# Hybrid decoder layer: the recurrence's tanh, exponentials and square roots laid in a row on ScalarE

## The chip, the cores and the metric

The kernel runs on one core of one Trainium2 chip. The metric is device time in microseconds (us), the median of the runs. Engines are named as in the profile: PE is TensorE, ACT is ScalarE, DVE is VectorE, POOL is GpSimd and SP is the engine that issues the DMAs.

## The reference

One decoder layer on a residual stream of 2048 tokens of width 1024, with 16 meta tokens put in front (T = 2064). Both groups of heads read one projection, and one output projection joins them:

```python
u = rmsnorm(h, pre_g)
q, k, v, g_att, x_lru, g_lru = split(u @ w_in)          # six blocks of 1024 columns
att = rmsnorm(stick_breaking_attention(q, k, v), att_out_g) * silu(g_att)
lru = rmsnorm(rglru_branch(x_lru, ...), lru_out_g) * silu(g_lru)
y = concatenate([att, lru]) @ w_out
return h + rmsnorm(y, post_g)

# rglru_branch: after a causal convolution of width 4 gives xc
r = sigmoid(gate_a(xc)); i = sigmoid(gate_x(xc))
log_a = 8 * r * log_sigmoid(lru_lambda)
a = exp(log_a)
b = sqrt(-expm1(2 * log_a)) * (i * xc)
h_t = a_t * h_(t-1) + b_t

# stick-breaking attention, 8 heads of 128
z = q k' / sqrt(128);  w = the product over later keys of sigmoid(-z), split at each key;  o = w v
```

## The kernel before, in words

The work goes through 8 rounds, called heads here, 0 to 7. Round h holds attention head h and block h of 128 recurrence channels. Products on TensorE are made of three f16 matmuls (high x high, high x low, low x high), and so every projection is evicted twice: ACT writes the high half (`kH`, `qH`, line 792), then DVE subtracts it and writes the low half (`kL`, `qL`, line 796).

A projection is cut in chunks of columns: for k and v 144, 384, 512, 512, 512, for q 128, 384, 512, 512, 512. A chunk is 24 matmuls into one PSUM bank `mm`, of which there are three (`psm`, with `bufs=3`, `Ring(3)` in the planner). A bank is free again when its low half has been written. The two gate matmuls of the recurrence (L379 and L380) and the small matmul that scales a weight (L152) use the same three banks.

Attention cuts the 16 query tiles of a head into 26 segments of up to 1024 key columns. Each goes through: scores on PE (`z`, L219, two PSUM buffers), sigmoid on ACT (L223), a mask on POOL (L228), a running product on DVE (L233), a high half on ACT (`w`, L243 and L245), a low half on DVE (L250 and L251), a DMA transpose into `wT`, and the output matmuls on PE (`o`, L270).

The mix of block c is the elementwise part of the recurrence. It works on two halves (m = 0, 1) of HT = 1032 columns each: `tanh` (L390), `exp_a` (L393), `exp_a2` (L397, in place of its own input) on ACT, `rest` on DVE (L402: (exp_a2 + 1) x tanh), `sqrt` on ACT (L406), `drive` on POOL (L410), `recur`, a scan, on DVE (L414), `square` on ACT (L418) and `add` on POOL (L424 for the first block, L426 for the others). Mix c starts after the 12 gate matmul pairs of block c, and from mix 1 on this falls into the time in which PE makes k and q of head c. Tanh and sigmoid are in one of ACT's tables here, the exponential in another and the square root in a third; a change between them is an instruction of its own, ACT_TABLE_LOAD.

The order on PE, ACT and DVE is written out beforehand by a planner (class `Plan`, function `weave`). It keeps a model time for each engine (`plan.free`), adds a modelled duration for each step (`A` for ACT, `V` and `SC` for DVE, `G` for POOL) and calls a step's function, which emits its instructions, when the model time of PE reaches the time that the step was put down for (`plan.at`). The order of the calls is the order on every engine, since each takes its instructions in order. The planner's own times are only its model; they set the order and nothing else.

Of the kernel before, what the change touches and what calls it, by code (L numbers as in the profile page):

```python
# [70 lines left out]
def hybrid_layer(nc, tc, I, out):  # L71
# [221 lines left out]
    HT = T // 2  # L293
# [325 lines left out]
    plan = Plan()  # L619
    A = lambda t, n, table=None: plan.run("act", t, 0.2 + n / 1200, table)  # L620
# [393 lines left out]
    def gate_in(c, m, k, t):  # L1014
        def go():
            head[c]["mix"].gate_in(m, k)
            t2 = V(A(max(t, plan.free["pe"]), 344), 400)
            urgent.append((t2 + 1.2, rmm, lambda: out(t2)))

        def out(t2):  # L1020
            mix = head[c]["mix"]
            def emit():
                mix.gate_out(m, k)
                t3 = PE(0, 2 * 344)
                rcs[k % 2].put(t3)
                t4 = A(A(t3, 344, "sig"), 344, "sig")
                rmm.put(t4)
                if k == 5:
                    G(t4, HT)
                head[c]["gates"] += 1  # L1030
                if k + 2 < 6:
                    plan.at(t3, lambda: gate_in(c, m, k + 2, t3))
                if head[c]["gates"] == 6 and "conv1" in head[c]:
                    plan.at(t4, head[c].pop("conv1"))
                if head[c]["gates"] == 12:
                    plan.at(t4, lambda: rows_for(len(mix.xs), lambda: mix_end(c)))
            emit()
        rcs[k % 2].get(go)
# [4 lines left out]
    def mix_end(c):  # L1043
        mix = head[c]["mix"]
        n = len(mix.xs)
        now = lambda: plan.free["pe"]

        def tanh(m):
            mix.tanh(m)
            t = A(now(), HT, "tanh")  # L1050
            plan.at(t, (lambda: tanh(m + 1)) if m + 1 < n else (lambda: exp(0)))

        def exp(i):
            m = i // 2
            (mix.exp_a2 if i % 2 else mix.exp_a)(m)
            t = A(now(), HT, "exp")
            if i % 2:
                plan.at(t, lambda: rest(m))
            if i + 1 < 2 * n:
                plan.at(t, lambda: exp(i + 1))  # L1060

        def rest(m):
            mix.rest(m)
            t = V(now(), HT)
            rrow.put(t)
            if m + 1 == n:
                plan.at(t, lambda: sqrt(0))

        def sqrt(m):
            mix.sqrt(m)  # L1070
            t = A(now(), HT, "sqrt")
            plan.at(t, lambda: drive(m))
            if m + 1 < n:
                plan.at(t, lambda: sqrt(m + 1))

        def drive(m):
            mix.drive(m)
            t = G(now(), HT)
            plan.at(t, lambda: recur(m))

        def recur(m):
            mix.recur(m)
            t = SC(now(), HT)
            rlrow.put(t)
            if m + 1 == n:
                head[c]["hs"] = mix.xcs
            plan.at(t, lambda: square(m))

        def square(m):
            mix.square(m)  # L1090
            t = A(now(), HT)

            def add():
                mix.add(m)
                rrow.put(G(t, HT))
            plan.at(t, add)
        tanh(0)


    wos, nout, held, first_out = [], [0], [], []  # L1100
# [421 lines left out]
```

## Time and profile before

| what | value |
|---|---|
| time, median of 3 runs | 1884.48 us (1883.8 to 1887.8) |
| the profiled execution's own time | 1882.98 us |
| its span, first to last instruction | 1881.1 us |
| mean granted TensorE clock | 0.989 |
| busy: PE, DVE, ACT, POOL | 95%, 68%, 56%, 18% of the span |
| ACT_TABLE_LOAD | 46, of 1.283 us each |
| DMA | 108 GB/s on average |

The profiled execution is 1.5 us below the median of the runs and 0.8 us below the fastest of the three; what is read from its rows holds for its own 1882.98 us. Busy shares are means over stages with different limits. An engine's idle time has a cost only where PE waits for it, so the waits of PE are what is looked for.

### The profile page before, as it was taken

What the parts mean: (1) busy time and instruction counts of PE and PEld (TensorE: products, weight loads), DVE (VectorE), ACT (ScalarE), POOL (GpSimd) and SP (SyncE); (2) the same over time, 40 slices, a digit from 0 to 9 for tenths busy, and PEclk for the clock granted to TensorE, in tenths of its full rate; (3) what the DMA queues carried; (4) which work ended last, traced back from release to release, by engine and by line L of the source; (5) the groups of instructions that cost most, each with busy time, mean ns of one, the idle gap of its engine ahead of it and who ended that gap; (6) DMA issues with size and microseconds to landing.
All of it is one profiled execution on the core that took longest, in us unless ns stands there. A gap on an engine that the chain in (4) does not pass through costs nothing. (4 is left out here: it accounts for less than half of the span.)

```text
span 1881.1 us, 30861 instructions
## 1 busy us (share of the span) xinstructions
PE 1795.0 (95%) x12104; PEld 1155.2 (61%) x12104; DVE 1282.7 (68%) x1759; ACT 1047.9 (56%) x1789; POOL 343.3 (18%) x442
## 2 busy tenths in 40 slices
PE   3987999999999999998999899999999999999998
PEld 2544665566556655664665466556655678888776
DVE  8747876987778668767885788687857851134553
ACT  7768557556655755665567546665565742233221
POOL 0013012311320131014101401241131000002222
PEclk8998999999999999999999999999999999999999
DMA  6713650654175226433652355145405884354553
GB/s 211 144 29 74 125 109 27 123 105 87 49 139 104 63 54 127 97 64 65 134 100 55 73 126 98 46 97 132 83 30 108 192 184 144 96 177 154 179 190 134
DMA packets 428417, 203.46 MB, mean 108 GB/s; under 512 B 362976, under 2 KB 396768, under 8 KB 428272
## 3 DMA queue, kind: packets, MB, share of 16 engines
q1 hardware_dynamic: 428272, 201.49, 45.9%
q8 instruction: 95, 1.56, 0.3%
q14 instruction: 50, 0.41, 0.1%
HBM read 78.23 MB, written 34.08 MB: 60 GB/s over the span
## 5 line engine op out<-in xcount | busy, mean ns | idle before, releaser
L174 PE MATMUL mm<-uH,wH 128*128 128x512 f16 (+3 forms) x1808 | 616.3, 345 | 8.3 <-DVE sa L892 2.6
L174 PE MATMUL mm<-uL,wH 128*128 128x512 f16 (+3 forms) x1808 | 616.3, 345 | 0.0
L174 PE MATMUL mm<-uH,wL 128*128 128x512 f16 (+3 forms) x1808 | 615.4, 345 | 0.8 <-DVE wL L163 0.8
L174 PEld LDWEIGHTS <-wH 128*128 128x128 f16 x3616 | 333.9, 98 | 273.1 <-issue 10.4
L233 DVE TENSOR_TENSOR_SCAN row<-row 128x656 f32<-128x656 f32 (+6 forms) x208 | 352.4, 1695 | 131.9 <-POOL row L228 101.5
L174 PEld LDWEIGHTS <-wL 128*128 128x128 f16 x1808 | 177.3, 98 | 158.5 <-DVE wL L163 1.3
L270 PE MATMUL o<-wT,v 128*128 128x128 f16 x3392 | 224.4, 220 | 30.0 <-DMA wT<-w 26.5
L270 PEld LDWEIGHTS <-v 128*128 128x128 f16 x3392 | 206.1, 98 | 70.4 <-issue 27.0
L223 ACT ACTIVATE row<-z,zs 128x656 f32<-128x656 f32 (+6 forms) x208 | 171.5, 825 | 125.2 <-PE z L219 115.0
L251 DVE TENSOR_TENSOR w<-row,w 128x640 f16<-128x640 f32 (+5 forms) x208 | 179.8, 865 | 16.3 <-ACT w L245 14.4
L245 ACT CAST w<-row 128x640 f16<-128x640 f32 (+5 forms) x208 | 155.1, 746 | 51.8 <-DVE row L233 49.1
L537 PE MATMUL y<-woH,aH 128*128 128x512 f32 x352 | 140.8, 400 | 1.6 <-DVE w L251 1.6
L537 PE MATMUL y<-woH,aL 128*128 128x512 f32 x352 | 138.7, 394 | 0.5 <-DVE aL L530 0.5
L537 PE MATMUL y<-woL,aH 128*128 128x512 f32 x352 | 138.3, 393 | 0.6 <-DVE woL L490 0.6
L228 POOL TENSOR_SCALAR_AFFINE_SELECT row<-row 128x128 f32<-128x128 f32 x128 | 59.9, 469 | 406.4 <-ACT row L223 374.7
L219 PE MATMUL z<-kH,qH 128*128 128x328 f16 (+10 forms) x384 | 123.6, 322 | 0.6 <-ACT row L223 0.6
L219 PE MATMUL z<-kL,qH 128*128 128x328 f16 (+10 forms) x384 | 123.5, 322 | 0.0
L219 PE MATMUL z<-kH,qL 128*128 128x328 f16 (+10 forms) x384 | 123.4, 321 | 0.0
L219 PEld LDWEIGHTS <-qH 128*128 128x128 f16 x768 | 72.8, 98 | 56.3 <-issue 3.7
L369 DVE TENSOR_TENSOR cs<-lrow,cs 64x344 fp32r<-64x344 f32 x96 | 50.7, 528 | 78.5 <-ACT cs L368 71.3
L530 DVE TENSOR_TENSOR aL<-araw,aH 128x1024 fp32r<-128x1024 f32 x32 | 39.4, 1231 | 93.2 <-ACT aH L527 92.1
L1468 POOL TENSOR_TENSOR row<-row 128x512 f32<-128x512 f32 x32 | 46.5, 1454 | 262.9 <-ACT row L1467 251.1
(208 smaller groups left out, 2476.2 us busy)
## 6 DMA issues: line engine op xcount, KB each, us to landing
wraw<-in_w_in SPq DMA_DIRECT2D x45, 512.0 KB, 3.5
row<-in_x SPq DMA_DIRECT2D x22, 512.0 KB, 3.8
aa_d<-sa SPq DMA_DIRECT2D x34, 256.0 KB, 2.0
al_d<-sl SPq DMA_DIRECT2D x32, 256.0 KB, 2.4
araw<-in_w_out SPq DMA_DIRECT2D x16, 512.0 KB, 4.4
araw<-al_d SPq DMA_DIRECT2D x16, 512.0 KB, 4.3
yl_d<-ys SPq DMA_DIRECT2D x32, 256.0 KB, 2.1
row<-yl_d SPq DMA_DIRECT2D x16, 512.0 KB, 3.2
```

What stands on the lines that cost most here:

```text
L174: pe.matmul(out=ps[:, :n], lhsT=a[:, kt, :], rhs=b[:, kt, c0:c0 + n], start=(k == 0), stop=(k == 3 * KT - 1))
L219: pe.matmul(out=z[:, a, :n], lhsT=l[:, qs], rhs=r[:, c], start=(x == 0), stop=(x == 2))
L223: act.activation(out=self.om[:, :L].rearrange("p (a c) -> p a c", a=self.parts), in_=self.z[:, :self.parts, :self.n], func=AF.Sigmoid, sca ...
L228: pool.affine_select(out=d, in_=d, pattern=[[-1, P]], compare_op=ALU.is_gt, fill=1.0, base=0, channel_multiplier=1)
L233: dve.tensor_tensor_scan(out=om, data0=om, data1=om, initial=self.pred.om[:, 0:1] if self.si else WS, op0=ALU.mult, op1=ALU.bypass)
L245: act.copy(out=w[:, r0:r0 + nb * P], in_=om[:, self.m0:self.L])
L251: dve.tensor_tensor(out=w[:, r0 + nb * P:r0 + 2 * nb * P], in0=om[:, self.m0:self.L], in1=w[:, r0:r0 + nb * P], op=ALU.subtract)
L270: pe.matmul(out=o[:, c], lhsT=l, rhs=r, start=(self.si == 0 and x == 0), stop=(self.last and x == len(prods) - 1))
L369: dve.tensor_tensor(out=cs[oth, :n], in0=xc[own, a:a + n], in1=cs[own, :n], op=ALU.subtract)
L530: dve.tensor_tensor(out=aL, in0=raw, in1=aH, op=ALU.subtract)
L537: pe.matmul(out=ps, lhsT=a[:, c, :], rhs=b[:, 512 * half:512 * half + 512], start=(c == 0 and x == 0), stop=(c == KT - 1 and x == 2))
L1468: pool.tensor_tensor(out=yt[:, cs], in0=yt[:, cs], in1=pg[:, cs], op=ALU.mult)
```

## The change

The six steps of tanh and exponentials of a mix, which the planner emitted one at a time, each after the modelled end of the one before, are now emitted together: tanh of both halves, then both exponentials of both halves. The two square roots also follow each other at once, after the second half's `rest`. Nothing is added or taken out but table loads: by the built program there are 38 ACT_TABLE_LOAD where there were 46. The planner runs with the new steps, so its order differs everywhere from mix 0 on.

```diff
-        def tanh(m):
-            mix.tanh(m)
-            t = A(now(), HT, "tanh")
-            plan.at(t, (lambda: tanh(m + 1)) if m + 1 < n else (lambda: exp(0)))
-
-        def exp(i):
-            m = i // 2
-            (mix.exp_a2 if i % 2 else mix.exp_a)(m)
-            t = A(now(), HT, "exp")
-            if i % 2:
-                plan.at(t, lambda: rest(m))
-            if i + 1 < 2 * n:
-                plan.at(t, lambda: exp(i + 1))
+        def tables():
+
+            for m in range(n):
+                mix.tanh(m)
+                A(now(), HT, "sig")
+            for m in range(n):
+                mix.exp_a(m)
+                mix.exp_a2(m)
+                t = A(A(now(), HT, "exp"), HT)
+                plan.at(t, lambda m=m: rest(m))
 
         def rest(m):
             mix.rest(m)
             t = V(now(), HT)
             rrow.put(t)
             if m + 1 == n:
-                plan.at(t, lambda: sqrt(0))
-
-        def sqrt(m):
-            mix.sqrt(m)
-            t = A(now(), HT, "sqrt")
-            plan.at(t, lambda: drive(m))
-            if m + 1 < n:
-                plan.at(t, lambda: sqrt(m + 1))
+                plan.at(t, sqrt)
+
+        def sqrt():
+            for m in range(n):
+                mix.sqrt(m)
+                t = A(now(), HT, "sqrt")
+                plan.at(t, lambda m=m: drive(m))
...
-        tanh(0)
+        tables()
```

On ACT in mix 0 (the first head, attention already running) the program had, from the first exponential on:

```order
L393 ACT_TABLE_LOAD
L393 ACTIVATE lrow<-row,nsp_m 128x1032
L223 ACT_TABLE_LOAD
L223 ACTIVATE row<-z,zs 128x528
L397 ACT_TABLE_LOAD
L397 ACTIVATE row<-row,nsp_m_76 128x1032
L161 ACTIVATE wH<-wraw,wm 128x1024
L243 CAST w<-row 128x2x16
L245 CAST w<-row 128x512
L393 ACTIVATE lrow<-row,nsp_m 128x1032
L223 ACT_TABLE_LOAD
L223 ACTIVATE row<-z,zs 128x656
```

It now has in that place:

```order
L393 ACT_TABLE_LOAD
L393 ACTIVATE lrow<-row,nsp_m 128x1032
L397 ACTIVATE row<-row,nsp_m_76 128x1032
L393 ACTIVATE lrow<-row,nsp_m 128x1032
L397 ACTIVATE row<-row,nsp_m_76 128x1032
L243 CAST w<-row 128x2x16
L245 CAST w<-row 128x384
L223 ACT_TABLE_LOAD
L223 ACTIVATE row<-z,zs 128x528
L161 ACTIVATE wH<-wraw,wm 128x1024
L406 ACT_TABLE_LOAD
L406 ACTIVATE row<-row 128x1032 x2
```

The four exponentials stand together. The first half of a segment's weights (`w`, 384 columns), which stood ahead of the first exponential, and the sigmoid of 528 columns, which stood behind it, now stand behind the fourth. Over the whole program mix 0 has 10 loads before and 4 now, mix 1 has 6 and 4, and mixes 2 to 7 have three each before and now.

On ACT in mix 4, from the last gate's sigmoids (L381, L382) on, before:

```order
L381 ACTIVATE row<-mm,pp 64x344
L382 ACTIVATE lrow<-mm,pp 64x344
L390 ACTIVATE row<-row,nsp 128x1032
L792 ACTIVATE kH<-mm 128x512
L390 ACTIVATE row<-row,nsp 128x1032
L792 ACTIVATE qH<-mm 128x128
L393 ACT_TABLE_LOAD
L393 ACTIVATE lrow<-row,nsp_m 128x1032
L792 ACTIVATE qH<-mm 128x384
L397 ACTIVATE row<-row,nsp_m_76 128x1032
L393 ACTIVATE lrow<-row,nsp_m 128x1032
L397 ACTIVATE row<-row,nsp_m_76 128x1032
```

And now:

```order
L381 ACTIVATE row<-mm,pp 64x344
L382 ACTIVATE lrow<-mm,pp 64x344
L390 ACTIVATE row<-row,nsp 128x1032 x2
L393 ACT_TABLE_LOAD
L393 ACTIVATE lrow<-row,nsp_m 128x1032
L397 ACTIVATE row<-row,nsp_m_76 128x1032
L393 ACTIVATE lrow<-row,nsp_m 128x1032
L397 ACTIVATE row<-row,nsp_m_76 128x1032
L792 ACTIVATE kH<-mm 128x512
L792 ACTIVATE qH<-mm 128x128
L792 ACTIVATE qH<-mm 128x384
L406 ACT_TABLE_LOAD
```

The evictions of the last k chunk (`kH`, 512 columns) and of the first two q chunks (`qH`, 128 and 384), which stood singly between the steps, now stand behind all six. Mixes 3, 5 and 7 have the same rows in this place now; in mix 6 the `kH` stands ahead of the six and a `qH` of 512 columns behind them; in mix 1 and mix 2 one `qH` of 512 columns stands first behind them.

On DVE in mix 4, from the low half of the k chunk before the last on, before:

```order
L796 SCALAR_TENSOR_TENSOR kL<-mm,kH 128x512
L195 TENSOR_SCALAR zs<-wm 128x1
L796 SCALAR_TENSOR_TENSOR kL<-mm,kH 128x512
L796 SCALAR_TENSOR_TENSOR qL<-mm,qH 128x128
L146 TENSOR_REDUCE wm<-wraw 128x1
L149 TENSOR_SCALAR dg<-identb,wm 128x128
L796 SCALAR_TENSOR_TENSOR qL<-mm,qH 128x384
L402 SCALAR_TENSOR_TENSOR row<-row 128x1032
```

And now:

```order
L796 SCALAR_TENSOR_TENSOR kL<-mm,kH 128x512
L195 TENSOR_SCALAR zs<-wm 128x1
L402 SCALAR_TENSOR_TENSOR row<-row 128x1032
L146 TENSOR_REDUCE wm<-wraw 128x1
L149 TENSOR_SCALAR dg<-identb,wm 128x128
L402 SCALAR_TENSOR_TENSOR row<-row 128x1032
L796 SCALAR_TENSOR_TENSOR kL<-mm,kH 128x512
L796 SCALAR_TENSOR_TENSOR qL<-mm,qH 128x128
L796 SCALAR_TENSOR_TENSOR qL<-mm,qH 128x384
```

The low half of the last k chunk stood ahead of both `rest` steps (L402), and now stands behind both. On PE the order of the chunks is the same in both programs there (last k chunk, then q of 128, 384, 512, 512, 512); behind the last gate pair stand 12 matmuls of the last k chunk before and 9 now in mix 4 (9 in mixes 3 and 5 too, 12 in mix 7). The first matmul of the first q chunk of 512 columns waits for the bank of the last k chunk, so for that chunk's `kL`, in both programs.

## Rows read from the trace of the kernel before

**Rows 1.** The page, section 1: busy us (share of the span) xinstructions of TensorE.

```profile
PE 1795.0 (95%) x12104; PEld 1155.2 (61%) x12104; DVE 1282.7 (68%) x1759; ACT 1047.9 (56%) x1789; POOL 343.3 (18%) x442
```

**Rows 2.** Busy time by stretch: us, busy us (x) per engine, clock, DMA.

```profile
850.00:950.00 100.00, 94.82 (x693) 56.18 (x692) 80.91 (x111) 52.82 (x102) 26.24 (x37) 1.00 0.52 104
```

**Rows 3.** Groups of ScalarE instructions: busy us, mean ns, idle before.

```profile
L223 ACT ACT_TABLE_LOAD x15 | 19.2, 1283 | 0.3
...
L406 ACT ACT_TABLE_LOAD x10 | 12.8, 1283 | 0.2
```

**Rows 4.** Timeline of ScalarE around mix 4: start us, us, instruction, idle before.

```profile
833.11 0.54 ACT L382 ACTIVATE lrow<-mm,pp 64x344 f32<-64x344 f32 x1
833.67 1.15 ACT L390 ACTIVATE row<-row,nsp 128x1032 f32<-128x1032 f32 x1
835.14 0.60 ACT L792 ACTIVATE kH<-mm 128x512 f16<-128x512 f32 x1 [0.32 <-PE mm L174]
...
836.97 1.28 ACT L393 ACT_TABLE_LOAD   x1
838.26 1.16 ACT L393 ACTIVATE lrow<-row,nsp_m 128x1032 f32<-128x1032 f32 x1
...
840.77 1.15 ACT L397 ACTIVATE row<-row,nsp_m 128x1032 f32<-128x1032 f32 x1
841.82 1.14 ACT L393 ACTIVATE lrow<-row,nsp_m 128x1032 f32<-128x1032 f32 x1
842.99 1.15 ACT L397 ACTIVATE row<-row,nsp_m 128x1032 f32<-128x1032 f32 x1
...
847.47 1.06 ACT L406 ACTIVATE row<-row 128x1032 f32<-128x1032 f32 x1
...
849.48 1.05 ACT L406 ACTIVATE row<-row 128x1032 f32<-128x1032 f32 x1
```

**Rows 5.** Timeline of VectorE around mix 4.

```profile
835.77 0.69 DVE L796 SCALAR_TENSOR_TENSOR kL<-mm,kH 128x512 f16<-128x512 f32 x1 [2.56 <-ACT kH L792]
...
837.19 1.21 DVE L146 TENSOR_REDUCE wm<-wraw 128x1 f32<-128x1024 f32 x1
...
841.95 1.23 DVE L402 SCALAR_TENSOR_TENSOR row<-row 128x1032 f32<-128x1032 f32 x1 [0.49 <-ACT row L397]
```

**Rows 6.** Timeline of TensorE: the first matmul of three projection chunks.

```profile
834.94 0.22 PE L174 MATMUL mm<-uH,wH 128*128 128x128 f16 x1
...
836.28 0.33 PE L174 MATMUL mm<-uH,wH 128*128 128x384 f16 x1
...
840.18 0.38 PE L174 MATMUL mm<-uH,wH 128*128 128x512 f16 x1
```

**Rows 7.** Timeline of GpSimd at the start of head 4.

```profile
857.72 3.84 POOL L426 TENSOR_TENSOR acc_l<-acc_l,row 128x1016 f32<-128x1016 f32 x1 [1.02 <-ACT row L418]
...
861.88 2.38 POOL L426 TENSOR_TENSOR acc_l<-acc_l,row 128x1032 f32<-128x1032 f32 x1
864.21 0.61 POOL L228 TENSOR_SCALAR_AFFINE_SELECT row<-row 128x128 f32<-128x128 f32 x2
```

**Rows 8.** Waits of TensorE, 500 to 1450 us: us in total, times, longest us.

```profile
PE o L270 <- DMA wT<-w: 15.2, 11, 2.8
PE o L270 <- ACT sq L285: 3.4, 1, 3.4
```

**Rows 9.** Busy time by stretch at the starts of heads 3 and 5.

```profile
700.00:704.40 4.40, 2.43 (x22) 1.41 (x21) 0.52 (x2) 0.69 (x2) 0.41 (x2) 1.00 0.50 98
704.40:707.80 3.40, 3.40 (x10) 1.20 (x9) 3.40 (x6) 1.99 (x5) 0.00 (x0) 0.50 0.00 0
...
1070.00:1085.00 15.00, 10.87 (x82) 6.25 (x81) 14.51 (x21) 10.18 (x21) 6.18 (x6) 1.00 0.73 131
```

**Rows 10.** Timeline of ScalarE in mix 0.

```profile
146.03 1.16 ACT L390 ACTIVATE row<-row,nsp 128x1032 f32<-128x1032 f32 x1 [1.25 <-DVE w L251]
...
151.49 0.70 ACT L223 ACTIVATE row<-z,zs 128x528 f32<-128x528 f32 x1
```

## The prediction

> **What bounds the kernel now.** The page's first section comes first: TensorE is busy for 95% of the span, ScalarE for 56%, VectorE for 68% [rows 1]. ScalarE, whose work the change rearranges, is therefore not the bound over the whole. To see whether it is one in a stage, read the busy time by stretch: in the first half of head 4 TensorE is busy for 94.82 of 100 us and ScalarE for 52.82 [rows 2]. So two questions decide. Where does TensorE wait now, and does the new order take such a wait away? And does it make a new one in a place where TensorE now runs through?
>
> **Table loads.** A load takes 1.283 us, whichever table it is [rows 3], and the instruction behind it starts at once: the load at 836.97 ends at 838.25, the exponential starts at 838.26 [rows 4]. Eight loads fewer are 8 x 1.283 = 10.3 us of ScalarE's time, all of it in mixes 0 and 1. In mixes 2 to 7 there are three loads before and three after, so there the change moves work and saves none. An engine that is 56% busy gives time to the end only where TensorE waits for it, and I book these 10.3 us as nothing by themselves; their cover is TensorE's own work in the first two heads. What they would be worth without it is a rival below.
>
> **The new stall, mixes 3, 4, 5 and 7.** The last k chunk is evicted by `kH` on ScalarE and `kL` on VectorE, and only `kL` gives back its bank, which the first q chunk of 512 columns takes again three chunks later. Before, `kH` stood between the two tanh (835.14) [rows 4], `kL` came at 835.77 [rows 5], and that q chunk started at 840.18 [rows 6] with the bank long free.
>
> Now `kH` stands behind all six activations. Taking mix 4's own times: the group starts at 833.67, where the first tanh does, right behind the last gate's sigmoid (833.11 + 0.54). Two activations in a row are 1.05 us apart when the second doesn't need the first (840.77 to 841.82), and 1.17 us when it does, as `exp_a2` needs `exp_a` (841.82 to 842.99); the last takes 1.15, the load 1.28 [rows 4]. So the group takes 1.05 + 1.15 + 1.28 + 1.17 + 1.05 + 1.17 + 1.15 = 8.0 us and ends at 841.7. `kH` (0.60) ends at 842.3. VectorE meanwhile has the first `rest` from 839.5, when the first `exp_a2` ends, the 1.21 us reduction of a weight, the second `rest` (1.23 each) [rows 5], and only then `kL`: 839.5 + 1.23 + 1.21 + 1.23 + 0.69 = 843.9.
>
> When does TensorE want the bank? A chunk of 384 columns is 24 matmuls and takes 840.18 - 836.28 = 3.90 us [rows 6], so TensorE does 24 x 384 / 3.90 = 2360 columns per us, and a matmul of 512 takes 0.217 us. With 9 instead of 12 k matmuls behind the last gate pair it arrives 0.65 us earlier than the old 840.18, at 839.5. It waits for 843.9 - 839.5 = 4.3 us in mixes 3, 4 and 5, and for 3.7 us in mix 7, which still has the 12. If `kL` is not held by the `rest` steps, the wait is until 842.3 + 0.69 = 843.0, 3.5 us; that is the lower bound. The upper bound has one more attention step of the size of a low half (0.69) ahead of `kL`: 5.0 us. In mix 6 `kH` is ahead of the group and only a 512-column `qH` is behind it; a whole 512-column chunk (5.2 us) plus the two small ones cover nearly all of it, and I take 0.8 us. In mixes 1 and 2 it is a single `qH` whose bank has over 10 us of chunks in front of it: nothing; without that cover each would cost up to the same 4.3. **Term 1: 3 x 4.3 + 3.7 + 0.8 = +17.4 us.** Queued behind the late `kH` are the `qH` of 128 and 384 columns; the chunks that need their banks come 5.2 us later, so they add nothing.
>
> **Mix 0.** The sigmoid of 528 columns at 151.49 [rows 10] moves behind all four exponentials: the second tanh ends at 147.2 [rows 10], a load (1.28) and the four (1.17 + 1.05 + 1.17 + 1.15) end at 153.0; then two weight casts (about 0.6 together, as the `kH` of like size in [rows 4]) and a load, so it starts at 154.9, 3.4 us later. It frees the score buffer that the next scores need. Against it the mix has six loads fewer, 7.7 us of ScalarE. I take **+2 us** (-2 to +4). The moved steps issue no DMA in any mix; only the transposes of `w` follow their casts.
>
> **The clock.** A stall of 4 us may also lower TensorE's granted clock. At the start of head 3 it was idle for 1.97 of 4.40 us, and in the next 3.40 us, fully busy, it had 0.50, the lower level of 1.2 GHz: a loss of 1.7 us. At the start of head 5 it was idle for 4.1 of 15 us, in pieces, and kept 1.00 [rows 9]. So an idle piece costs sometimes. I take six in ten of the four stalls, 4 x 0.6 x 1.7 = 4.1, less the old fall at head 3, which should go (next term): **+2.4 us**, bounds -1.7 and +6.8. The Trainium skill, page "TensorE: Matmul & The Clock Gate", section "Part 1: The HAM clock gate", states that the throttled clock is the default and that idling brings it back; by that every one of the four stalls would be charged, +6.8. The trace agrees for head 3 and disagrees for head 5.
>
> **What is given back.** TensorE's waits between 500 and 1450 us are mostly at the starts of heads: output matmuls that wait for the transpose of `w`, 15.2 us in 11 waits, and one of 3.4 us at a square [rows 8]: 18.6 us. One reason is the tail of the mix. The adds of the recurrence's squares on POOL run from 857.72 to 864.26, and the head's first masks stand behind them at 864.21 [rows 7]; a mask, a product, a cast and the transpose come ahead of the first output matmul. After the change the second `rest` ends at 843.2; the evictions are done by then, and a load and both square roots (1.05 each) run from about 843.5 to 846.9, against 850.5 before [rows 4]. The tail is some 3.6 us earlier, while TensorE, held by the stall, reaches the head's scores 4 us later. Against that tail the adds are out of the masks' way. What speaks against a full recovery: the wait is for a chain of four engines, of which the adds are one link. I take **-13 us** of the 18.6 (bounds 0 and -18.6).
>
> **Sum:** 17.4 + 2 + 2.4 - 13 = +8.8 us on the profiled execution's 1882.98 us (its span of 1881.1 and 1.9 around it): 1891.8. The median of the three runs is 1.5 us above that execution, and would give 1893.3; I predict 1892.
>
> **The rivals.** A difference under 0.2%, some 3.8 us, is about what a measurement of this kernel can tell from none.
>
> (a) The stall only moves idle time. Every microsecond that TensorE waits in mid-head lets the other engines run ahead, and the head-start waits are 18.6 us large: then -18.6 stands against 17.4, the clock and mix 0 add 0 to 4, and the time is about 1884. For it: the sizes are alike. Against it: the waits are not all in the heads that get a stall.
>
> (b) Faster. The bank comes back at 843.0 because `kL` isn't held by the `rest` steps, so the four stalls are 3.5, 3.5, 3.5 and 2.9 = 13.4; the head-start waits and head 3's clock fall vanish, -20.3; mix 0 is even. That is -7, 1876. It decides as soon as more comes back than the stalls take, about 17 us with mine. Against it: VectorE's row of instructions puts `kL` behind both `rest` steps.
>
> (c) Faster by the loads. If ScalarE were on TensorE's path all through mixes 0 and 1, their eight loads would come off, -10.3, and with stalls and recovery cancelling the time is about 1873. For it: all eight are in these two mixes. Against it: ScalarE itself waited 1.25 us ahead of the second tanh of mix 0 [rows 10], so it had time over, and the sigmoid there is put back, not forward. The Trainium skill, page "ScalarE: Activation LUTs", section "Table sets: the hidden batching unit", tells to batch activations by table set, and its section "What ACT_TABLE_LOAD costs" puts a switch at 1283 ns and a drain of about 1380 ns; by those figures the eight are an estimated 21 us. The trace agrees with the load and shows no drain before the next start.
>
> (d) Nothing comes back: the waits at head starts are for something else than the adds, for example VectorE's running products. Then +17.4 + 2 + 4.1 = +23.5, 1907.
>
> That the change does nothing is excluded: the loads are 38 instead of 46, and the rows of three engines differ.
>
> **How the numbers follow.** My forecast has 0.50, with 1888 to 1898 as its own range; (a) 0.20, (b) 0.08, (c) 0.04, (d) 0.18. Faster is (b) and (c), 0.12; same is (a), 0.20; slower is the forecast and (d), 0.68. The range leaves out (b), (c) and the far part of (d), together under 2 in 10: 1880 to 1903. Its ends are the sum with recovery complete and mix 0 at its lower bound (17.4 - 2 - 18.6 + 0 = -3.2, 1880), and the sum with no more than a quarter of the recovery (17.4 + 2 + 4.1 - 4 = +19.5, 1903).
>
> **What the profile of the changed kernel would show.** Term 1: waits of TensorE on the projection's line for `kL`, four of about 4 us, in mixes 3, 4, 5 and 7; on ScalarE, six activations with one load between tanh and exponentials, `kH` behind them. Mix 0: a later sigmoid of 528 columns and a wait of the scores behind it. The clock: stretches at 0.50 behind the stalls. The give-back: fewer and shorter waits of output matmuls for `wT` at the head starts, adds of squares that end before the first mask. Loads: 38. I am wrong if the stalls are there and the waits at the head starts are untouched (then 1907), if they vanish altogether (1884 or less), or if the q chunk doesn't wait at all.

## The result, and the profile after

| what | before | after |
|---|---|---|
| time, median of 4 runs each | 1885.2 us (1883.8 to 1887.8) | 1908.4 us (1907.2 to 1911.6) |
| ratio, 95% interval | | 1.0123 (1.0108 to 1.0138) |
| profiled execution, its span | 1882.98, 1881.1 us | 1908.76, 1907.0 us |
| mean granted TensorE clock | 0.989 | 0.982 |
| ACT_TABLE_LOAD | 46 | 38 |

The change costs 23 us where 8.8 were forecast, and the time lies above the range. Up to mix 0 the two programs are the same, yet the first tanh of mix 0 starts at 143.64 us before and at 145.96 after, and up to there the same 662 matmuls kept TensorE busy for 104.9 and for 107.4 us. So 2.3 of the 25.9 us between the two spans belong to the two executions and 23.6 to the change; the medians differ by 23.2.

The page of the changed kernel, section 1, answers to [rows 1]:

```profile
PE 1807.2 (95%) x12104; PEld 1160.2 (61%) x12104; DVE 1265.6 (66%) x1759; ACT 1040.1 (55%) x1781; POOL 339.0 (18%) x442
```

ScalarE's busy time is 7.8 us shorter (1047.9 to 1040.1), less than the eight loads of 1.283 us that are gone (10.3). TensorE is busy for 12.2 us more with the same 12104 instructions, which is its clock: 2.4 of the 12.2 lie ahead of mix 0, where the programs are the same, and 9.8 come with the change. Some waits of TensorE over the whole span (us in total, times, longest), before:

```profile
PE o L270 <- DMA wT<-w: 26.5, 17, 5.1
...
PE mm L174 <- ACT lrow L382: 2.3, 3, 1.7
...
PE mm L379 <- DVE kL L796: 1.4, 5, 0.3
...
PE z L219 <- ACT row L223: 0.6, 1, 0.6
```

And after:

```profile
PE mm L174 <- DVE kL L796: 16.6, 4, 4.3
...
PE o L270 <- DMA wT<-w: 12.9, 10, 5.0
...
PE mm L174 <- ACT lrow L382: 9.2, 7, 2.0
PE z L219 <- ACT row L223: 6.2, 2, 3.2
PE o L270 <- ACT ot L282: 3.4, 3, 1.1
...
PE mm L152 <- ACT lrow L382: 2.9, 4, 0.7
...
PE mm L152 <- DVE qL L796: 0.7, 1, 0.7
...
PE mm L174 <- DVE qL L796: 0.2, 1, 0.2
```

The wait of the q chunk for `kL` is new and is 16.6 us in four pieces. Waits for the gates' second sigmoid (L382) were 2.5 before and are 12.1. Scores waiting for a sigmoid were 0.6 and are 6.2. Output matmuls waited 29.9 before (26.5 for `wT`, 3.4 for a square) and now 16.3. Waits ahead of mix 2 for weights and gates of the output (L161, L163, L154, L892) shrank by 4.9. With 0.6 at L149 the sum is 16.6 + 9.6 + 5.6 - 13.6 - 4.9 + 0.6 = +13.9 of idle time; smaller waits take 0.2 off. With the 12.2 of slower matmuls that is the 25.9 us between the spans.

Mix 4 shows the stall. On VectorE, then ScalarE and TensorE (timelines: start, us, instruction, idle before):

```profile
852.00 1.23 DVE L402 SCALAR_TENSOR_TENSOR row<-row 128x1032 f32<-128x1032 f32 x1 [8.99 <-ACT row L397]
853.15 1.21 DVE L146 TENSOR_REDUCE wm<-wraw 128x1 f32<-128x1024 f32 x1
...
854.56 1.23 DVE L402 SCALAR_TENSOR_TENSOR row<-row 128x1032 f32<-128x1032 f32 x1
855.71 0.68 DVE L796 SCALAR_TENSOR_TENSOR kL<-mm,kH 128x512 f16<-128x512 f32 x1
```

```profile
846.10 2.20 ACT L390 ACTIVATE row<-row,nsp 128x1032 f32<-128x1032 f32 x2
848.33 1.28 ACT L393 ACT_TABLE_LOAD   x1
...
853.04 1.16 ACT L397 ACTIVATE row<-row,nsp_m 128x1032 f32<-128x1032 f32 x1
854.10 0.58 ACT L792 ACTIVATE kH<-mm 128x512 f16<-128x512 f32 x1
```

```profile
856.44 0.58 PE L174 MATMUL mm<-uH,wH 128*128 128x512 f16 x1 [4.31 <-DVE kL L796]
```

The group starts at 846.10 and ends at 854.20, 8.1 us later; `kH` follows, and `kL` comes behind both `rest` steps at 855.71. The first matmul of the q chunk of 512 columns waits 4.31 us for it. Before, the chunk did not wait: its bank had been free since 836.5, when `kL` ended [rows 5 and 6].

The gates, a little earlier in the same head, on TensorE and on ScalarE:

```profile
831.31 0.31 PE L380 MATMUL mm<-cs,gL 128*128 128x344 f32 x1
...
831.75 0.32 PE L380 MATMUL mm<-cs,gL 128*128 128x344 f32 x1
832.82 0.22 PE L152 MATMUL mm<-dg,onesb 128*128 128x128 bf16 x1 [0.74 <-ACT lrow L382]
835.06 0.38 PE L174 MATMUL mm<-uH,wH 128*128 128x512 f16 x1 [2.03 <-ACT lrow L382]
```

```profile
832.22 0.54 ACT L382 ACTIVATE lrow<-mm,pp 64x344 f32<-64x344 f32 x1
832.79 0.60 ACT L792 ACTIVATE kH<-mm 128x512 f16<-128x512 f32 x1
...
833.91 0.54 ACT L381 ACTIVATE row<-mm,pp 64x344 f32<-64x344 f32 x1
834.47 0.54 ACT L382 ACTIVATE lrow<-mm,pp 64x344 f32<-64x344 f32 x1
```

Two gate pairs stand side by side, right behind the last of the 24 matmuls of a k chunk. That chunk's bank still waits for its eviction, and the pairs take the two others. Their sigmoids give these back, and between the sigmoids of the two pairs ScalarE does a `kH` and a cast. The next two users of a bank wait 0.74 and 2.03 us. This happens in heads 3, 4 and 5. Gate pairs side by side are not new: the kernel before has them in heads 3, 5 and 7, but there behind 18 of a chunk's 24 matmuls, so that TensorE goes on with the six others in a bank that it already holds, and its one wait is 0.34 us.

Busy time by stretch (us, busy us of PE, PEld, DVE, ACT, POOL, granted clock, DMA): the stretches after 300 us that ran at the lower level.

```profile
342.20:345.60 3.40, 2.60 (x8) 1.13 (x8) 3.40 (x5) 2.24 (x6) 1.74 (x2) 0.50 0.71 83
646.00:649.40 3.40, 3.40 (x10) 1.18 (x8) 1.89 (x7) 1.25 (x2) 0.00 (x0) 0.50 0.00 0
666.50:673.30 6.80, 4.58 (x12) 1.68 (x12) 3.68 (x11) 5.12 (x7) 3.27 (x2) 0.50 0.00 0
854.20:861.00 6.80, 4.56 (x12) 1.68 (x12) 3.69 (x11) 5.12 (x7) 3.25 (x2) 0.50 0.00 0
1021.50:1024.90 3.40, 2.91 (x7) 0.99 (x7) 1.89 (x7) 2.03 (x3) 0.00 (x0) 0.51 0.00 0
1045.30:1048.80 3.50, 3.50 (x11) 1.30 (x10) 0.97 (x6) 2.37 (x3) 2.71 (x2) 0.51 0.01 2
1407.20:1414.00 6.80, 5.78 (x15) 2.12 (x15) 3.34 (x10) 4.28 (x4) 4.47 (x2) 0.50 0.01 2
```

Each lies at a wait: of scores (342), of gates in heads 3 and 5 (646, 1021; the same wait in head 4 has none), and at or behind all four stalls for `kL` (666, 854, 1045, 1407). In the stretch from 854.20 matmuls of 512 columns follow each other every 0.43 us, and right behind it every 0.22. So by estimate half of TensorE's busy time in the seven is lost: 13.7 us, of which (4.58 + 4.56 + 3.50 + 5.78) / 2 = 9.2 go with the stalls. Before, there were two such stretches after 300 us: the fall of [rows 9] at head 3, the only one between 500 and 1450 us, and one at 1489 us, with 6.56 us of busy time in all, so 3.3 us.

What comes back stands at the head starts. TensorE's output waits from 500 to 1450 us, which answer to [rows 8], and GpSimd at the start of head 4, which answers to [rows 7]:

```profile
PE o L270 <- DMA wT<-w: 4.7, 7, 1.3
PE o L270 <- ACT ot L282: 3.4, 3, 1.1
```

```profile
866.92 3.81 POOL L426 TENSOR_TENSOR acc_l<-acc_l,row 128x1016 f32<-128x1016 f32 x1 [1.01 <-ACT row L418]
870.93 2.36 POOL L426 TENSOR_TENSOR acc_l<-acc_l,row 128x1032 f32<-128x1032 f32 x1 [0.20 <-ACT row L418]
...
878.10 0.29 POOL L228 TENSOR_SCALAR_AFFINE_SELECT row<-row 128x128 f32<-128x128 f32 x1 [1.32 <-ACT row L223]
```

18.6 us have become 8.1. The adds now end at 873.3, and the first mask of the head, at 878.10, waits for its sigmoid alone. Both halves of the reason that the prediction gave can be read here, counted from the first tanh of mix 4: the last add ended 30.6 us behind it and now ends 27.2 behind it, and the head's first scores came 24.1 us behind it and now come 30.2. So the adds ended 6.5 us behind the scores and now end 3.0 ahead of them; 3.4 of these 9.5 us are the shorter tail, and 6.1 are TensorE's lateness.

### The profile page after: what moved, and what is told of

It reads as the page before. It is cut to its first block, busy times and chain, and to the rows that moved or that the text cites. A ratio compares the mean times of both kernels' runs of the same rounds, so it can differ in the third digit from the quotient of the medians.

```text
span 1907.0 us, 30849 instructions
## 1 busy us (share of the span) xinstructions
PE 1807.2 (95%) x12104; PEld 1160.2 (61%) x12104; DVE 1265.6 (66%) x1759; ACT 1040.1 (55%) x1781; POOL 339.0 (18%) x442
## 5 line engine op out<-in xcount | busy, mean ns | idle before, releaser
L174 PE MATMUL mm<-uH,wH 128*128 128x512 f16 (+3 forms) x1808 | 622.7, 348 | 28.5 <-DVE kL L796 16.6
L174 PEld LDWEIGHTS <-wH 128*128 128x128 f16 x3616 | 338.8, 99 | 307.3 <-issue 43.9
L270 PE MATMUL o<-wT,v 128*128 128x128 f16 x3392 | 223.4, 219 | 16.6 <-DMA wT<-w 12.9
L251 DVE TENSOR_TENSOR w<-row,w 128x640 f16<-128x640 f32 (+5 forms) x208 | 177.9, 858 | 17.6 <-ACT w L245 15.6
L245 ACT CAST w<-row 128x640 f16<-128x640 f32 (+5 forms) x208 | 154.8, 746 | 35.8 <-DVE row L233 30.8
L228 POOL TENSOR_SCALAR_AFFINE_SELECT row<-row 128x128 f32<-128x128 f32 x128 | 65.8, 516 | 426.5 <-ACT row L223 367.5
```

What stands on the lines that cost most here:

```text
L174: pe.matmul(out=ps[:, :n], lhsT=a[:, kt, :], rhs=b[:, kt, c0:c0 + n], start=(k == 0), stop=(k == 3 * KT - 1))
L228: pool.affine_select(out=d, in_=d, pattern=[[-1, P]], compare_op=ALU.is_gt, fill=1.0, base=0, channel_multiplier=1)
L245: act.copy(out=w[:, r0:r0 + nb * P], in_=om[:, self.m0:self.L])
L251: dve.tensor_tensor(out=w[:, r0 + nb * P:r0 + 2 * nb * P], in0=om[:, self.m0:self.L], in1=w[:, r0:r0 + nb * P], op=ALU.subtract)
L270: pe.matmul(out=o[:, c], lhsT=l, rhs=r, start=(self.si == 0 and x == 0), stop=(self.last and x == len(prods) - 1))
```

## The experiments

Two theories of the loss are tested. Theory A: the loss is the late `kH` and the bunched gates, with the clock falls that they bring, while loads saved are worth nothing. Theory B: rows of one table, or what mixes 0 and 1 do, set the time by themselves. On what is given back at the head starts, theory A adds that the mix's tail ends earlier, and theory C says that TensorE only comes later. The kernels from `noadd` on test why the head starts wait: theory A2 says that the squares and adds of a mix stand in the way of the head's first segments, and theory D that other work does as well. Times are medians, and ratios are to the kernel before.

**early**: the rows in mixes 0 and 1 alone.

```diff
+        SINGLE = c >= 2
...
-        tables()
+        tanh(0) if SINGLE else tables()
```

> The rows of tanh, exponentials and square roots are laid together in mixes 0 and 1 alone (40 loads), mixes 2 to 7 keep the single steps of before. Theory A (the loss sits in the waits of TensorE for the late evictions of k and for the gates, in heads 3, 4, 5 and 7; the loads saved are worth nothing): no wait for kL over 1 us, no new clock fall after 500 us, and only the 5 us that mixes 0 and 1 lost in the changed kernel, so 1888 to 1892. Theory B (ScalarE's loads in mixes 0 and 1 do lie on TensorE's path): 10 us faster, 1873 to 1878.

Measured: 1897.0 us, ratio 1.0065 (1.0053 to 1.0077). Both numbers missed. No q chunk waits for `kL`, but the clock falls after 500 us, which was not expected:

```profile
708.00:714.80 6.80, 5.29 (x23) 2.77 (x23) 3.71 (x7) 4.64 (x11) 1.71 (x4) 0.50 0.75 146
899.10:902.50 3.40, 3.04 (x20) 2.22 (x21) 3.21 (x5) 2.58 (x5) 3.16 (x3) 0.50 0.80 153
1083.40:1086.90 3.50, 3.50 (x13) 1.71 (x12) 3.26 (x3) 1.12 (x3) 2.10 (x2) 0.51 0.74 133
1264.30:1271.20 6.90, 5.68 (x29) 3.62 (x30) 5.94 (x6) 3.40 (x7) 4.37 (x4) 0.51 1.11 155
```

By the same estimate they cost 17.5 / 2 = 8.8 us, against 1.7 before, and the output waits from 500 to 1450 us are 22.4 instead of 18.6: 3.8 + 7.1, most of the 12.8 us between the spans of the two profiled executions (1893.9 and 1881.1). They lie at the starts of heads 3 to 6, whose own mixes are laid singly as before. The planner, begun otherwise, puts the later heads in another order: the first scores of head 4 come 22.8 us behind its first tanh, and before 24.1. Their waits come in longer pieces (4.6, 3.4, 3.0, 3.4) than before (2.8 the longest but for one of 3.4). That the new order is what made the pieces longer is argued; no run shows it apart.

**late**: the reverse (`SINGLE = c < 2`).

> The reverse: mixes 0 and 1 as before, the rows together in mixes 2 to 7 alone (46 loads, none saved). Theory A: the four waits for kL of 3.7 to 4.3 us are all there, with a clock fall behind each; the gate waits of 2.8 us come in heads 4 and 5, but not in head 3, whose gates have the spacing of before; head starts still give back some 13 us. 1899 to 1905. Theory B (the loss comes from mixes 0 and 1, and all later heads are only pushed): 1884 to 1890.

Measured: 1900.7 us, 1.0084 (1.0071 to 1.0097), as A says. All four waits for `kL` are there (15.9 us in all), gate waits in heads 4 and 5 and none in head 3, a clock fall at or behind each of the four, and output waits of 7.6. So most of the loss comes with the rows in mixes 2 to 7, where not one load is saved. `early` and `late` lose 11 and 15 us, together more than the change's 23: the long head-start waits of `early` are not in the changed kernel.

**sqrts**: only the square roots in a row.

```diff
-        def sqrt(m):
-            mix.sqrt(m)
-            t = A(now(), HT, "sqrt")
-            plan.at(t, lambda: drive(m))
-            if m + 1 < n:
-                plan.at(t, lambda: sqrt(m + 1))
+        def sqrt():
+            for m in range(n):
+                mix.sqrt(m)
+                t = A(now(), HT, "sqrt")
+                plan.at(t, lambda m=m: drive(m))
```

> Tanh and exponentials singly as before, only the two square roots in a row. No stall for kL is expected by either theory. Theory A (the head starts improve because the tail of the mix, and so the adds of squares on GpSimd, end earlier): the waits of output matmuls between 500 and 1450 us fall from 18.6 to 13 us or less, and the time to 1876 to 1882. Theory C (they improved only because TensorE itself came later, held by its stalls, and the others had caught up): they stay at 16 to 20 us, and the time at 1883 to 1888.

Measured: 1892.5 us (1888.8 to 1896.5), 1.0040 (1.0027 to 1.0053), with 42 loads, and the output waits from 500 to 1450 us rose:

```profile
PE o L270 <- DMA wT<-w: 23.0, 11, 4.6
```

Neither number held. The reason that A gave isn't met here: the tail didn't end earlier (the last add of mix 4 ends 30.8 us behind the first tanh, and before 30.6). The second scan of mix 4 ends 1.6 us behind the head's first scores in this kernel and in the one before, since it stands behind the first scan on VectorE and does not wait for the square root. So this run says nothing on what a shorter tail would give. Waits of 3.4 to 4.6 us in one piece brought clock falls at the starts of heads 3 to 6 here too; why the pieces grew stays open.

**pairs**: the six steps in three groups, evictions let in between.

```diff
-            for m in range(n):
-                mix.exp_a(m)
-                mix.exp_a2(m)
-                t = A(A(now(), HT, "exp"), HT)
-                plan.at(t, lambda m=m: rest(m))
+            plan.at(plan.free["act"], lambda: exps(0))
+
+        def exps(m):
+            mix.exp_a(m)
+            mix.exp_a2(m)
+            t = A(A(now(), HT, "exp"), HT)
+            plan.at(t, lambda: rest(m))
+            if m + 1 < n:
+                plan.at(t, lambda: exps(m + 1))
```

> As the changed kernel (38 loads), but the six steps are given out in three groups (two tanh; exponentials of the first half; of the second), each when the modelled ScalarE has ended the one before, so that the k and q evictions stand between them. Theory A: kH waits behind at most one tanh, kL comes ahead of both rest steps, so no wait for kL, and no clock fall in heads 3 to 7 but for a gate wait of 2.8 us in head 3 (the one head with gates bunched as in the changed kernel). Time 1878 to 1891, depending on how much the head starts give back without a stall. Theory B or any theory by which rows of one table are slower in themselves: over 1895.

Measured: 1885.9 us, 1.0002 (0.9993 to 1.0010): no change, with all eight loads gone, and in A's range. Its waits from 500 to 1450 us:

```profile
PE o L270 <- DMA wT<-w: 14.9, 9, 3.2
PE mm L174 <- ACT lrow L382: 2.0, 1, 2.0
```

No q chunk waits for `kL`. Gate pairs stand side by side in heads 3 to 7, but only in head 3 behind 24 of a chunk's matmuls, and there alone the gate wait comes; in heads 4 to 7 they stand behind 18 and cost 0.4 us. One clock fall more than expected lies at the start of head 3. Without stalls most of the output waits are back. That is C's part: much of the give-back came with the lateness.

**rest1**: the changed kernel with `kL` between the two `rest` steps.

```diff
-                plan.at(t, lambda m=m: rest(m))
+                plan.at(t + 2.0, lambda m=m: rest(m))
```

> The changed kernel, with the rest steps given out 2 us later, so that on VectorE the low half of the last k chunk stands between the two rest steps, not behind both, in mixes 3, 4, 5 and 7. Theory A: the wait for kL shrinks from 4.3 (3.7 in mix 7) to the time at which ScalarE's kH allows it, 3.4 to 3.5 (2.8 to 2.9), so 3.4 us in all; the gate waits of 2.8 us in heads 3, 4 and 5 stay; 1902 to 1906. If the clock falls behind those stalls hang on their length, up to 8 us more come off, 1895 to 1902. Rival: something else on TensorE's side holds it just as long, 1906 to 1910.

Measured: 1905.1 us (1903.8 to 1914.4), 1.0112 (1.0092 to 1.0131). The waits, and VectorE in mix 4:

```profile
PE mm L174 <- DVE kL L796: 12.6, 4, 3.3
```

```profile
851.27 1.23 DVE L402 SCALAR_TENSOR_TENSOR row<-row 128x1032 f32<-128x1032 f32 x1 [3.38 <-ACT row L397]
853.99 0.69 DVE L796 SCALAR_TENSOR_TENSOR kL<-mm,kH 128x512 f16<-128x512 f32 x1 [1.48 <-ACT kH L792]
...
855.26 1.22 DVE L402 SCALAR_TENSOR_TENSOR row<-row 128x1032 f32<-128x1032 f32 x1
```

`kL` now waits for `kH` itself, and the stalls are 3.3, 3.3, 3.3 and 2.7, 0.1 below what A expected. In heads 3 and 5 the clock held at 1.00 behind them; in heads 4 and 7 it fell. The time lies in A's range, but its interval overlaps that of the changed kernel (1.0108 to 1.0138), so that the time is shorter is not shown; the stalls are.

**delay15**: the row of six 1.5 us later, behind the last `kH`.

```diff
-        tables()
+        plan.at(now() + 1.5, tables)
```

> The changed kernel with its six steps given out 1.5 us later in the planner's time, so that kH of the last k chunk stands ahead of them, and the two small q evictions behind all six; its gates are spaced as in heads 4 and 6 of before. 38 loads. Theory A (the loss is the late kH, the bunched gates and the clock falls they bring): no wait for kL, no gate wait over 1 us in heads 3 to 7, no clock fall in mid-head; the waits at head starts are back at 3 to 6 us each, since TensorE comes early again; 1881 to 1892. Theory B (eight us of ScalarE in one piece hold TensorE wherever they stand): a wait of 3 us or more for a q eviction in each mix, over 1896.

Measured: 1882.6 us, 0.9983 (0.9975 to 0.9992). The whole row is there, and from 500 us on no q chunk waits for `kL` and nothing waits for gates: the 26 us between it and the changed kernel are what their order costs. So the rows of B fall; its mixes 0 and 1 are left to `lsq20`. After 500 us three clock falls remain, all at the starts of heads 4 to 6. The output waits from 500 to 1450 us are less than the 3 to 6 us a head that were expected:

```profile
PE o L270 <- DMA wT<-w: 12.8, 5, 3.3
```

TensorE has no stall here, so its lateness is not the whole of the give-back. In mix 4 the last add ends 27.2 us behind the first tanh, as early as in the changed kernel, and the scores come at 22.4, earlier than before. With that shorter tail 18.6 us of waits are 12.8, and with the lateness too, in the changed kernel, 8.1. The orders differ elsewhere as well, so this share is read from the traces and not isolated.

**noadd**: the kernel before, without the squares and adds of mixes 2 to 6. It leaves out part of the sums that the output is normalised by, so only its time and its order are of use.

```diff
-            mix.square(m)
+            if c not in (2, 3, 4, 5, 6):
+                mix.square(m)
...
-                mix.add(m)
+                if c not in (2, 3, 4, 5, 6):
+                    mix.add(m)
```

> The kernel before, with the squares (L418) and the adds (L426) of the recurrence left out in mixes 2 to 6, all other instructions in the same order; the sums of squares it normalises by are then wrong, and it is run for its time alone. Theory A2 (at a head's start the first sigmoids and masks stand behind these squares and adds, and that makes the outputs late): the waits of output matmuls from 500 to 1450 us fall from 18.6 to 9 us or less, and the time by 8 us or more, to 1871 to 1878. Theory D (they are one link of a chain that other work, the recurrence's scans and the v block's evictions, sets as well): 13 to 18 us of waits stay, and 1881 to 1887.

Measured: 1872.6 us, 0.9924 (0.9910 to 0.9937), 14 us faster:

```profile
PE o L270 <- DMA wT<-w: 7.0, 4, 2.1
```

Both numbers lie where A2 expected them: the head-start waits do hang on squares and adds. Two clock falls remain, at the starts of heads 4 and 5, behind waits of about 2 us.

**psq20, bsq20, dsq20, asq20**: the squares of mixes 2 to 6, and so the adds, 20 us later, in `pairs`, in the kernel before, in `delay15` and in the changed kernel. **lsq20** is `dsq20` with mixes 0 and 1 laid singly.

```diff
-            plan.at(t, lambda: square(m))
+            plan.at(t + (20.0 if 1 < c < H - 1 else 0.0), lambda: square(m))
```

> The three groups of the kernel pairs, and the squares and adds of mixes 2 to 6 given out 20 us later, behind the first segments of the head. Theory A2: the head-start waits of output matmuls fall to 9 us or less between 500 and 1450 us without any stall in mid-head, and it is faster than both kernels, 1873 to 1880. Theory D: the waits stay or move to the later segments, 1883 to 1890.

> The kernel before, its steps of tanh, exponential and square root singly as they were, and only the squares and adds of mixes 2 to 6 given out 20 us later (46 loads). Theory A2 (the head starts are set by where the squares and adds stand, whatever the tables do): the output matmuls' waits from 500 to 1450 us fall from 18.6 to 9 us or less, 1875 to 1881. Rival (it needs the shorter rows as well): 1883 to 1888.

> The kernel delay15 (all six steps in one row, 1.5 us later, behind kH; 38 loads) with the squares and adds of mixes 2 to 6 given out 20 us later. Theory A2: no wait for kL, and head-start waits of 9 us or less, so 4 to 9 us below delay15's 1882.6: 1873 to 1879. Rival (without idle time to spare the late adds collide with later masks): 1881 to 1887.

> The changed kernel itself with the squares and adds of mixes 2 to 6 given out 20 us later. Theory A2 with C (its stalls already let the adds end before the head's first masks, so there is little left to win): the four waits for kL stay, and the time within 5 us of the changed kernel, 1903 to 1910. Rival (late squares win by themselves, 7 us as from pairs to psq20): 1898 to 1902.

> As dsq20 in mixes 2 to 7, but mixes 0 and 1 with their steps singly as before: 46 loads, so the eight loads are not saved. Theory A (those loads are hidden, worth nothing): within 4 us of dsq20. Theory B (they are worth their 10.3 us or a good part): 6 to 10 us slower than dsq20.

| kernel | time, us | ratio to before, interval | output waits, 500 to 1450 us |
|---|---|---|---|
| psq20 | 1878.5 | 0.9954 (0.9942 to 0.9967) | 9.2 |
| bsq20 | 1878.6 | 0.9965 (0.9952 to 0.9977) | 10.8 |
| dsq20 | 1883.4 | 0.9990 (0.9981 to 0.9999) | 12.1 |
| asq20 | 1908.7 | 1.0132 (1.0114 to 1.0151) | 9.4 |
| lsq20 | 1881.9 | 0.9981 (0.9973 to 0.9990) | 11.9 |

`psq20` and `bsq20` are the fastest that compute everything, and alike, though one has 38 loads and the other 46. Their times lie where A2 expected them, and their output waits of 9.2 and 10.8 us just miss its 9. `asq20` gains nothing, as A2 with C expected: the changed kernel's stalls had already let the adds pass. `dsq20` missed A2's range and lies in its rival's: its output waits hardly fell (12.8 to 12.1 us), and a q eviction stands behind the row, for which TensorE waits in five heads:

```profile
PE mm L174 <- DVE qL L796: 4.7, 5, 0.9
```

`lsq20`, with the eight loads back, is no slower than `dsq20` (1.5 us faster), as A expected. From the first tanh of mix 0 to that of mix 2 TensorE waits for 18.0 us in `lsq20` and for 17.7 in `dsq20`.

## Why the prediction was wrong

**What bounds the kernel**, and that the loads saved are worth nothing by themselves, was right: `lsq20` against `dsq20`, and `pairs`, which has all eight gone and the time of before.

**Term 1** was right in place and size: +17.4 forecast, and 16.6 measured for `kL`, 4.3 in mixes 3, 4 and 5 and 3.7 in mix 7. In mix 6, where 0.8 was booked, TensorE waited 0.71 and 0.25 us for a `qL`. The reading there was not quite right: behind the six stand all of the `qH` of 128, 384 and 512 columns and not the last alone, and the longer wait is that of the matmul that scales a weight (L152). That `kL` also stands behind the `rest` steps, which rival (b) denied, is shown by `rest1`, which took 1.0 off each stall.

**What is given back** was of the right order: 13 of the 18.6 us between 500 and 1450 us forecast, 10.5 measured there, and 13.6 over the whole span. That squares and adds stand in the way is shown by `noadd` and `bsq20`. Of the two reasons given, the shorter tail and the later TensorE, both are in the trace (3.4 and 6.1 us in head 4), and `delay15`, which has only the first, gave 5.8 of the 10.5.

**The clock** is the first step that failed: "I take six in ten of the four stalls, 4 x 0.6 x 1.7 = 4.1". All four went with a fall, and a fall cost 1.8 to 2.9: 9.2 us. The row of head 5, four us of idle in pieces, was no model for one piece of four. The upper end of the range took the same 4.1. The Trainium skill's page "TensorE: Matmul & The Clock Gate", section "Part 1: The HAM clock gate", by which every one of these stalls is charged, was the better guide on how many (+6.8 by it); the trace agrees on four of four and shows a larger sum. Falls at the gates and at head 1's scores, (2.60 + 3.40 + 2.91) / 2 = 4.5 us, were in no term.

**A term was missing**, the second step that failed. I looked for new stalls only behind the group of six. The planner's new order also puts two gate pairs side by side behind a finished chunk in heads 3, 4 and 5; the waits for L382 are 9.6 us longer, 8.3 of it there. The cost goes with the place and not with the bunching: in all the kernels here, from head 3 on, such pairs behind 24 matmuls of a chunk cost 2.8 us each time (11 of 11), and behind 18 at most 0.4 (28 of 28). The order of TensorE showed where the pairs stand, and the count of three banks would have priced them.

**Mix 0** was booked at +2. The expected wait of scores behind the later sigmoid came (3.2 us), with one of 3.0 in mix 1 that I had booked at nothing; 4.9 us of weight waits went in exchange, so 0.7 of idle time is left. `lsq20` against `dsq20`, where the row starts later, puts the net at about +1.5.

| term | forecast, us | measured, us |
|---|---|---|
| stalls behind the six | +17.4 | +17.6 |
| waits for gates | 0 | +9.6 |
| mixes 0 and 1, idle time | +2 | +0.7 |
| clock | +2.4 | +9.8 |
| output waits | -13 | -13.6 |
| other waits | 0 | -0.5 |
| together | +8.8 | +23.6 |

The clock and the gates, 7.4 + 9.6 over the forecast, are more than the whole difference of 14.8. Rival (d) gave 1907 and came nearest, but for a wrong reason: it had nothing coming back, and 13.6 us did. Open is what the `kH` between the gates' sigmoids adds to the place of the pairs; no kernel here takes it away alone.

## What to carry to other kernels

Grouping activations by table saves loads, and was worth nothing here, where TensorE sets the end; the price is what the row puts off on ScalarE's queue. Before laying a row, look for the evictions that it would delay, count the PSUM banks in front of their next user, and put the row behind them (`delay15`, 26 us better than the change). Look also at where the new order puts small users of the same banks: inside a chunk they cost next to nothing, at its end 2.8 us. And an accumulation that nobody needs soon, here squares and adds, is worth moving out of the way of a new stage's first links: 20 us later it gave 7 us in two kernels (`bsq20` without touching the tables, and `psq20` against `pairs`), and nothing in two others (`dsq20`, `asq20`).

## What was not expected of the hardware

A wait can cost TensorE more than its length, by a price that jumps. The stalls of 3.7 to 4.3 us in one piece each went with a stretch at the lower clock level, 0.50 (eight of eight in the changed kernel and `late`), at 1.8 to 2.9 us apiece in the changed kernel by estimate. Shorter ones went either way: two of `rest1`'s 3.3, 3.3, 3.3 and 2.7 were followed by one, and so was a wait of 2.1 us in `noadd` (885 us), but not one of 3.4 us in the kernel before (1075 us). Idle time in short pieces brought no fall: `dsq20` and `lsq20` have 12 us of output waits and 4.7 of q waits between 500 and 1450 us, none longer than 1.6, and no such stretch there. So in `early` 3.8 us more of head-start waits came with 7.1 us of slower matmuls. And the identical start of the program took between 143.6 and 146.9 us up to the first tanh of mix 0 in the fourteen executions profiled here.
